# Seven Strassen products for the sv projection, its move to the end of the projections, and rotary swaps and decay powers moved off VectorE

## The chip, the cores and the metric

The kernel runs on one core of one Trainium2 chip. Its time is the device time of one execution in microseconds. The core's engines are TensorE (PE, with its weight loads listed as PEld), VectorE (DVE), ScalarE (ACT), GpSimd (POOL) and SyncE (SP), whose queue issues most transfers. Each works through its own instructions in order and waits for the others at semaphores.

## The reference

The kernel computes one layer of a hybrid encoder for 512 positions of width 1024, in float32. The part that the change touches is the first half of it, the projections, the retention and the spatial gating unit (SGU):

```python
h = rmsnorm(x, g_pre_mix)
q, k, v, g, u, sv, a_ret, a_sgu = split(h @ w_in)     # widths 512, 512, then 1024 each
# rotary, per head of 128 columns (64 + 64)
q = concat([t1 * cos - t2 * sin, t1 * sin + t2 * cos]) # the same for k
# retention, 4 heads, in both directions with decays gamma_f, gamma_b
#   o[n] = sum over m <= n of gamma_f^(n-m) (q[n].k[m]) v[m] + sum over m > n of gamma_b^(m-n) (q[n].k[m]) v[m]
y_ret = (layernorm_per_head(o) * silu(g)) @ w_ret_o
sv = layernorm(gelu(sv))
y_sgu = (gelu(u) * (w_spatial applied to sv per 128 positions + b_spatial)) @ w_sgu_o
x1 = x + rmsnorm((sigmoid(a_ret) * y_ret + sigmoid(a_sgu) * y_sgu) @ w_out)
y = x1 + rmsnorm(conv_gated_mlp(rmsnorm(x1)))
```

## The kernel before

**Products in three matmuls.** Every float32 product is made of three matmuls in a reduced format: each operand is split into a high half, a copy on ScalarE (`copy`, line 95), and a low half, the operand less its high half, on VectorE (`split`, line 112); then high·high, high·low and low·high are added up in a PSUM bank of 128 x 512. There are eight such banks.

**The weights' stream.** `units` lists the weight blocks in the order in which the products want them, written out by hand. `raw_tile` gives one of four tiles of 128 x 1024, which a transfer on the SP queue fills from `wall` (512 KB); `slot` gives one of nine weight slots ("w4") for a half. `w_get` hands out the next unit and prepares later ones as far as its look-ahead (`LOOK`, 4) and the slots allow. A block (`w_block`) is split in one go of 1024 columns. For Strassen products `w_form` (lines 177 to 202) makes forms of 512 columns from two loaded blocks: T1 to T4 are sums and differences in a further raw tile (lines 188, 189, 191, 194), and each form is split into its own slot. The copy on ScalarE and the low half on VectorE stand in the engines' queues among everything else, and a raw tile can be loaded anew when its last reader is done.

**The stages.** First q and k (all eight banks, lines 346 to 376), with x in high and low halves. Their raw results go to SBUF (lines 446 to 452), cos and sin are loaded on the SP queue (lines 468, 469) and scaled on VectorE (470, 471). Then `t_group` (lines 563 to 576) makes one 512-column half of v, sv or g for all four blocks of 128 rows: 4 weight blocks x 4 row blocks x 2 x 3 = 96 matmuls of 128 x 512 (lines 573 to 575), with a `yield` after each weight block. Half 0 of v comes first, beside head 0's preparation. Then the loop over the four heads runs one `t_group` each, interleaved with a head: transposes of k (`k_rows`, line 552), `scores` (line 600), after the first weight block `states`, after the second `prep` of the next head and `values` (line 629), then the other two weight blocks and the evacuation. The groups are v half 1, sv half 0, sv half 1, g half 0. A fifth group makes g half 1; in it the first half of the retention's output, multiplied by its gate, is transposed (`transposed`, line 698), and x's forms for k = 2, 3 are made (`x_forms`, lines 377 to 390). sv's normalization (`sv_norm`, line 685) and the second gate (`g_evac`, lines 707, 708) follow.

**Retention on VectorE.** `rotary` (lines 511 to 517) makes four instructions, two of which read the other 64 partitions (lines 514, 515). `powers` (lines 502 to 508) makes a matrix of decays of 128 x 512 with two VectorE instructions (lines 504, 505) and one exponential on ScalarE, once for `scores` and once for q's factor xi. `o` is normalized per head after a square root on GpSimd (line 657).

**U and the gates.** u comes in four Strassen pairs (class `Pair`, products on line 793): seven products of 12 matmuls with 256 columns for a pair of output blocks, with the products M1 and S2 in one bank, whose content is copied out by ScalarE between them. The first pair takes its products in the order M1, S1, S2, and then the second term of M1's output. The second half of the retention's output is transposed in the first gated pair (`last_turn`, line 715). Gates, output projection and the convolution MLP follow, and are unchanged.

Of the kernel before, what the change touches and what calls it, by code (L numbers as in the profile page):

```python
# [27 lines left out]
U0, GATE0, GATE1 = 32, 40, 72  # L28
# [19 lines left out]
def tile_block(ctx: ExitStack, tc, xT, x, wall, par, cs, wsp, bsp, gpost, gffn, out):  # L48
# [72 lines left out]
    while i < NW:  # L121
        pair = [(f, i) for f in FORMS]
        if U0 <= i < GATE0:
# [17 lines left out]
        else:  # L141
            units.append(("blk", i))
            i += 1
    w_ready, w_pos, w_held, w_raw = {}, [0, 0], [0], {}
# [75 lines left out]

    def w_unit(u):
        return w_block(u[1]) if u[0] == "blk" else (w_down if u[0] in "qt" else w_form)(*u)

    def w_size(u):
        return 2 if u[0] in ("blk", "q", "t") else 1
# [196 lines left out]
    v = nc.vector  # L422
# [57 lines left out]
    (dp, dn), (xp, xn) = halves("dd"), halves("xx")  # L480

    def clip(o, i, op):
        v.tensor_scalar(out=o, in0=i, scalar1=0.0, scalar2=None, op0=op)

    iota(dp.rearrange("p (i n) -> p i n", i=2), [[-P, 2], [1, 256]], 0, -1)
    clip(dn, dp, ALU.min)
    clip(dp, dp, ALU.max)
    iota(xp, [[1, S]], -255, 0)
    iota(xn, [[1, S]], -256, 0)
    clip(xp, xp, ALU.max)  # L490
    clip(xn, xn, ALU.min)
# [10 lines left out]
    def powers(o, p, n, h):  # L502

        v.tensor_scalar(out=o, in0=p, scalar1=lg[:, h : h + 1], scalar2=None, op0=ALU.mult)
        v.scalar_tensor_tensor(
            out=o, in0=n, scalar=lg[:, 4 + h : 5 + h], in1=o, op0=ALU.mult, op1=ALU.add
        )
        nc.scalar.activation(out=o, in_=o, func=AF.Exp)
        return o

    def rotary(m):
        a, b = blk(n="rot"), tmp("rb")
        v.tensor_mul(a, raw[m], cosr)
        v.tensor_mul(b[0:64], raw[m][64:128], sinr[64:128])
        v.tensor_mul(b[64:128], raw[m][0:64], sinr[0:64])
# [21 lines left out]
    def prep(h):  # L537
# [5 lines left out]
        xi = powers(tmp("xi"), xp, xn, h)  # L543
# [56 lines left out]
    def scores(h):  # L600
        (qh, ql), (kh, kl) = hd[h][:2]
        dec = powers(tmp("dec"), dp, dn, h)
# [65 lines left out]
    def sv_evac(acc, nh):  # L668
        for t in range(NT):
            z = blk(n="sv")  # L670
            nc.scalar.activation(
                out=z, in_=acc[t], func=AF.Gelu_apprx_tanh, scale=rstd[:, t : t + 1]
            )
            v.bn_stats(out=sst[:, t, nh, :], in_=z)
            svz[t, nh] = z
        if nh == 1:
            for t in range(NT):
                v.bn_aggr(out=smv[:, t, :], in_=sst[:, t].rearrange("p a b -> p (a b)"))
            rsqrt(srstd, smv[:, :, 1], 1.0, NT)
# [13 lines left out]
    def transposed(src, hi, lo):  # L693

        for f in range(4):
# [7 lines left out]

    def g_evac(acc, nh):
        for t in range(NT):
            g = tmp("g")
            nc.scalar.activation(out=g, in_=acc[t], func=AF.Silu, scale=rstd[:, t : t + 1])
            v.tensor_mul(o_sb[t, nh], o_sb[t, nh], g)

    def last_turn(fs):  # L710

        for f in fs:
            p = ps()
            for t in range(NT):
                i = nc.tensor.transpose(p[:, t * P : (t + 1) * P], o_sb[t, 1][:, f * P : (f + 1) * P], ident)
            h_, l_ = blk(F32R, "gh"), blk(F32R, "gl")
            split(h_, l_, p)
            ogh.append(h_)
            ogl.append(l_)
        return i.ins  # L720
# [9 lines left out]

    for h in range(H):
        gen = t_group()
        k_rows(h)
        sm = scores(h)
        acc = next(gen)
        st = states(h)
        next(gen)
        if h + 1 < H:
# [12 lines left out]
    for n, acc in enumerate(t_group()):  # L751
# [764 lines left out]
```

## Time and profile before

| what | value |
|---|---|
| median of 3 runs | 790.97 us (789.35, 790.97, 791.0) |
| the profiled execution's own time | 791.37 us |
| its span in the profile | 789.6 us |
| granted TensorE clock, mean | 0.997 |
| q and k | to about 47 us |
| v half 0, and heads 0 to 2 with their groups | 48 to 152 us |
| head 3 and the g half 0, then g half 1 | 152.5 to 203 us |
| four U pairs | 203.3 us on |

A row of the groups of lines has the line, engine, operation, output and inputs, shapes and count, then the busy time in us, the mean ns of one and the idle time of the engine ahead of them with its releaser. A row of a timeline has the start and length in us, the engine, line and operation, and in brackets the idle time ahead of it and what ended it. A duration overlaps the next one's start on VectorE, ScalarE and PE, so the time that an instruction takes of its engine is read from start to start. Rows of windows have, after the stretch and its length, the busy time of PE, PEld, DVE, ACT and POOL with the number of instructions, then the granted clock, the share of the DMA engines and GB/s.

### The profile page before, as it was taken

To read this page: it belongs to the slowest core of one execution; us is meant where nothing else is said; L and a number is where in the kernel's file an instruction comes from. 1 tells how busy PE (TensorE), PEld (TensorE's weight loads), DVE (VectorE), ACT (ScalarE), POOL (GpSimd) and SP (SyncE) were. 2 spreads that over 40 slices of the span, in tenths; PEclk is the share of its full clock that TensorE was granted. 3 is DMA by queue.
4 is the path that set the end of the run, shared out by engine and by line. 5 is a ranking of instruction groups with operands and counts; after the bars stand their busy time and mean duration, and the time that the engine had idled before them with its cause. 6 is when DMAs were issued, how large, how long until landed. Compare 5 with 4: busy or idle time off the path is not lost.

```text
span 789.6 us, 13358 instructions
## 1 busy us (share of the span) xinstructions
PE 779.5 (99%) x5163; PEld 724.9 (92%) x5163; DVE 645.1 (82%) x1102; ACT 451.0 (57%) x805; POOL 88.0 (11%) x106
## 2 busy tenths in 40 slices
PE   9999999999999999999999999999999999999996
PEld 8888998998999999999998898999999998999996
DVE  7489998887897777777765669999999889877877
ACT  7546446645676444444444677657777578744442
POOL 0010000110001011032211210001111012200001
PEclk9999999999999999999999999999999999999998
DMA  8733222222233333233359111435555365633244
GB/s 298 264 124 107 80 82 79 81 81 70 104 108 107 107 107 107 86 103 107 134 164 339 59 54 54 116 111 141 141 147 147 108 192 120 168 109 116 99 161 161
DMA packets 33679, 99.54 MB, mean 126 GB/s; under 512 B 3984, under 2 KB 5904, under 8 KB 33616
## 3 DMA queue, kind: packets, MB, share of 16 engines
q1 hardware_dynamic: 27360, 86.76, 32.0%
q0 software_dynamic: 5392, 10.75, 6.4%
q10 hardware_dynamic: 864, 1.18, 0.4%
q8 instruction: 40, 0.66, 0.4%
q14 instruction: 23, 0.19, 0.1%
HBM read 88.19 MB, written 4.19 MB: 117 GB/s over the span
## 4 chain that ended last, share of the span: by engine, by line
PE 80%; DVE 8%; DMA 5%; ACT 3%; issue 2%; POOL 0%; SPq 0%; POOLq 0%; DVEq 0%; ACTq 0%
PE ps L793 23%; PE ps L242 10%; PE ps L241 10%; PE ps L243 10%; PE ps L1210 6%; PE ps L573 5%; PE ps L575 5%; PE ps L574 5%; DMA raw<-wall 3%; DVE dl L112 1%; DMA x<-x 1%; DMA xT<-xT 1%; PE ps L874 1%; PE ps L959 1%; PE ps L958 1%
## 5 line engine op out<-in xcount | busy, mean ns | idle before, releaser
L112 DVE TENSOR_TENSOR wl<-raw,wh 128x1024 fp32r<-128x1024 f32 (+1 forms) x92 | 105.7, 1157 | 41.5 <-PE ps L793 18.9
L95 ACT ACTIVATE wf<-raw 128x512 fp32r<-128x512 f32 x140 | 84.7, 624 | 81.4 <-PE ps L242 29.7
L793 PE MATMUL ps<-sh,wf 128*128 128x256 f32 x640 | 116.6, 275 | 0.0
L112 DVE TENSOR_TENSOR wf<-raw,wf 128x512 fp32r<-128x512 f32 x140 | 101.2, 735 | 18.6 <-ACT wf L95 18.1
L95 ACT ACTIVATE wh<-raw 128x1024 fp32r<-128x1024 f32 (+2 forms) x96 | 93.0, 980 | 24.2 <-DMA raw<-wall 13.1
L793 PEld LDWEIGHTS ps<-sh,wf 128*128 128x128 f32 x640 | 101.7, 192 | 0.5
L242 PE MATMUL ps<-h2l,wh 128*128 128x512 f32 (+1 forms) x256 | 90.2, 354 | 0.7 <-DVE h2l L1031 0.7
L243 PE MATMUL ps<-h2h,wl 128*128 128x512 f32 (+1 forms) x256 | 90.1, 353 | 0.0
L241 PE MATMUL ps<-h2h,wh 128*128 128x512 f32 (+1 forms) x256 | 90.1, 354 | 0.0
L793 PE MATMUL ps<-sl,wf 128*128 128x256 f32 x320 | 88.0, 275 | 0.0
L573 PE MATMUL ps<-wh,xh 128*128 128x512 f32 x192 | 73.0, 380 | 0.0
L574 PE MATMUL ps<-wl,xh 128*128 128x512 f32 x192 | 72.8, 379 | 0.0
L575 PE MATMUL ps<-wh,xl 128*128 128x512 f32 x192 | 72.8, 379 | 0.0
L793 PEld LDWEIGHTS ps<-sl,wf 128*128 128x128 f32 x320 | 61.4, 192 | 0.4
L1210 PE MATMUL ps<-dl,fh 128*128 128x256 f32 x216 | 59.6, 276 | 0.2 <-DVE dl L112 0.2
L1210 PE MATMUL ps<-dh,fh 128*128 128x256 f32 x216 | 59.4, 275 | 0.0
L1210 PE MATMUL ps<-dh,fl 128*128 128x256 f32 x216 | 59.4, 275 | 0.0
L95 ACT ACTIVATE dh<-raw 128x768 fp32r<-128x768 f32 (+1 forms) x36 | 33.6, 949 | 36.0 <-DVE raw L214 21.1
L242 PEld LDWEIGHTS ps<-h2l,wh 128*128 128x128 f32 x256 | 48.6, 190 | 5.4 <-DVE h2l L1031 0.9
L243 PEld LDWEIGHTS ps<-h2h,wl 128*128 128x128 f32 x256 | 48.5, 190 | 5.2
L793 PE MATMUL ps<-xh,wf 128*128 128x256 f32 x288 | 52.8, 277 | 0.0
L241 PEld LDWEIGHTS ps<-h2h,wh 128*128 128x128 f32 x256 | 48.4, 190 | 4.8 <-ACT h2h L1028 0.3
(317 smaller groups left out, 2045.2 us busy)
## 6 DMA issues: line engine op xcount, KB each, us to landing
raw<-wall SPq DMA_DIRECT2D x144, 512.0 KB, 3.5
x<-x SPq DMA_DIRECT2D x24, 256.0 KB, 6.1
fl<-gp POOLq DMA_DIRECT2D x12, 256.0 KB, 3.7
x<-x POOLq DMA_DIRECT2D x8, 256.0 KB, 2.4
fl<-fs POOLq DMA_DIRECT2D x8, 256.0 KB, 3.4
xT<-xT SPq DMA_DIRECT2D x7, 256.0 KB, 5.3
xT<-xT POOLq DMA_DIRECT2D x4, 256.0 KB, 3.3
fl<-gp POOLq DMA_DIRECT2D x8, 128.0 KB, 3.6
```

Source lines behind the costliest of these rows:

```text
L95: return nc.scalar.activation(out=o, in_=i, func=AF.Copy)
L112: nc.vector.tensor_sub(lo, src, as32(hi))
L241: nc.tensor.matmul(o, ah, bh, start=start, stop=False, skip_group_check=skip)
L242: nc.tensor.matmul(o, ah, bl, start=False, stop=False, skip_group_check=skip)
L243: nc.tensor.matmul(o, al, bh, start=False, stop=stop, skip_group_check=skip)
L573: nc.tensor.matmul(acc[t], xh[k][:, c], turns(wh[:, f]), start=k == 0, stop=False)
L574: nc.tensor.matmul(acc[t], xh[k][:, c], turns(wl[:, f]), start=False, stop=False)
L575: part_end[0] = nc.tensor.matmul(acc[t], xl[k][:, c], turns(wh[:, f]), start=False, stop=k == KD - 1)
L793: self.last = nc.tensor.matmul(o, w_[:, c], a_, start=first and k == n == 0, stop=k == 3 and n == 2, skip_group_check=True,)
L874: nc.tensor.matmul(o[:, t * P : (t + 1) * P], svz[t, j // 4][:, (j % 4) * P : (j % 4 + 1) * P], wst[:, gs], start=True, stop=True,)
L958: nc.tensor.matmul(o, ah, turns(bh), start=k == 0, stop=False)
L1210: nc.tensor.matmul(o, a_[:, c], turns(w_[:, f]), start=j == t == i == 0, stop=j == DP - 1 and i == 2 and n not in (M2, M3, M4), skip_group ...
```

## The change

- **sv by Strassen.** sv's 512 x 1024 by 1024 product is made of seven products instead of eight. `sv_group` takes seven products of 24 matmuls with 512 weight columns moving (x's forms are the stationary side): 168 matmuls instead of 192. Each product accumulates into two banks; three times the banks' content is saved by ScalarE and at the end added or subtracted on VectorE (`finish`). The weights' forms (`w_sv`) come from running sums: `s_sum` is loaded from two strided transfers of 256 KB and added to in place, and the forms are split in halves of 512, or 1024 at once for the three that stand in a raw tile.
- **Order.** v half 1, g half 0 and g half 1 come with heads 0 to 2; sv comes with head 3 and after it. g half 1 is kept in SBUF (`gate`) and multiplied after the loop. x's forms for k = 2, 3 come after heads 1 and 2. The transposes of the retention's output stand at three steps of sv's generator, and `last_turn` goes. `sv_norm` comes after the first U pair.
- **Rotary.** The exchange of the two halves of 64 partitions is done by 16 transfers of 128 KB on the SP queue, issued ahead of those of cos and sin, and a rotary has three instructions on VectorE. The sign of sin's table is turned accordingly.
- **Powers.** Distances stay unclipped where all of a block has one sign, and ScalarE makes the power by an exponential with a scale: four of 128 x 128 for a decay matrix, two of which read two small VectorE instructions, and two of 128 x 256 for xi.

```diff
-U0, GATE0, GATE1 = 32, 40, 72
+SV0, U0, GATE0, GATE1 = 24, 32, 40, 72
...
+        if i == SV0:
+            units += [(f, k) for f in ("s11", "sT1", "sT2") for k in range(2)]
+            units += [(f, k) for k in range(2) for f in ("s22", "sT3")]
+            units += [(f, k) for f in ("s21", "sT4") for k in range(2)]
+            i = U0
...
+    def w_sv(form, kp):
+
+        def load(n):
+            raw = raw_tile()
+            nc.sync.dma_start(raw, wall[SV0 + 2 * n + kp])
+            return raw
+
+        def add(raw):
+            for i in range(2):
+                v.tensor_add(s_sum[kp][i], s_sum[kp][i], raw[:, i * S : (i + 1) * S])
+
+        hi, lo = slot("sh"), slot("sl")
+        if form == "s11":
+            s_sum[kp] = halves("sb")
+            for i in range(2):
+                nc.sync.dma_start(s_sum[kp][i], wall[SV0 + kp, :, i * S : (i + 1) * S])
+        elif form == "sT1":
+            add(load(2))
+        elif form == "sT2":
+            s_22[kp] = load(3)
+            add(s_22[kp])
+        elif form == "s22":
+            split(hi, lo, s_22[kp])
+        elif form == "sT3":
+            raw = load(2)
+            v.tensor_add(raw, raw, s_22[kp])
+            split(hi, lo, raw)
+        elif form == "s21":
+            raw = load(1)
+            split(hi, lo, raw)
+            add(raw)
+        if form in ("s11", "sT1", "sT2", "sT4"):
+            for i in range(2):
+                f = slice(i * S, (i + 1) * S)
+                split(hi[:, f], lo[:, f], s_sum[kp][i])
+        return hi, lo
...
+    swapped = []
+    for m in range(8):
+        t = blk(n="swap")
+        for a, b in ((0, 64), (64, 0)):
+            nc.sync.dma_start(t[a : a + 64], raw[m][b : b + 64])
+        swapped.append(t)
...
+    def power(o, e, g):
+        nc.scalar.activation(out=o, in_=e, func=AF.Exp, scale=lg[:, g : g + 1])
+
+    def decays(h):
+
+        w, o = near[:, (2 + h % 2) * P : (3 + h % 2) * P], tmp("dec")
+        v.tensor_scalar(out=w, in0=near[:, :P], scalar1=lg[:, h : h + 1], scalar2=None, op0=ALU.mult)
         v.scalar_tensor_tensor(
-            out=o, in0=n, scalar=lg[:, 4 + h : 5 + h], in1=o, op0=ALU.mult, op1=ALU.add
+            out=w, in0=near[:, P : 2 * P], scalar=lg[:, 4 + h : 5 + h], in1=w, op0=ALU.mult, op1=ALU.add
         )
-        nc.scalar.activation(out=o, in_=o, func=AF.Exp)
+        q = o.rearrange("p (q n) -> p q n", q=4)
+        for i in (0, 3):
+            nc.scalar.activation(out=q[:, i], in_=w, func=AF.Exp)
+        power(q[:, 1], dist[:, 2 * P : 3 * P], h)
+        power(q[:, 2], dist[:, :P], 4 + h)
         return o
 
     def rotary(m):
-        a, b = blk(n="rot"), tmp("rb")
+        a, b = blk(n="rot"), swapped[m]
         v.tensor_mul(a, raw[m], cosr)
-        v.tensor_mul(b[0:64], raw[m][64:128], sinr[64:128])
-        v.tensor_mul(b[64:128], raw[m][0:64], sinr[0:64])
+        v.tensor_mul(b, b, sinr)
         v.tensor_add(a, a, b)
         return a
...
+    def sv_group():
...
+        def finish(n, bank, t0, nh, sub):
+            for t in range(2):
+                a, b = (bank[t], held[n][t]) if sub != "held" else (held[n][t], bank[t])
+                (v.tensor_sub if sub else v.tensor_add)(held[n][t], a, b)
+                gelu(t0 + t, nh, held[n][t])
+
+        b0 = [ps(), ps()]
+        yield from product(b0, x_(0, T0), True, False)
+        save("M1", b0, 0, 0)
+        b2 = [ps(), ps()]
+        yield from product(b2, s_("S1"), True, False)
+        save("M5", b2, 2, 1)
+        yield from product(b0, s_("S2"), False, False)
+        save("U2", b0, 0, 1)
+        for _ in zip(product(b2, s_("S4"), False, True), product(b0, s_("S3"), False, False)):
+            yield
+        finish("U2", b2, 0, 1, "bank")
+        finish("M5", b0, 2, 1, "held")
+        b1 = [ps(), ps()]
+        yield from product(b1, x_(4, T0), True, True)
+        finish("M1", b1, 0, 0, "")
+        yield from product(b0, x_(4, T1), False, True)
...
     for h in range(H):
-        gen = t_group()
+        gen = t_group() if h < 3 else sv_group()
...
-        for _ in gen:
-            pass
-        (v_evac, sv_evac, sv_evac, g_evac)[h](acc, (1, 0, 1, 0)[h])
+        if h < 3:
+            for _ in gen:
+                pass
+            (v_evac, g_evac, g_evac)[h](acc, (1, 0, 1)[h])
+        if h in (1, 2):
+            more_forms(h + 1)
+    for t in range(NT):
+        v.tensor_mul(o_sb[t, 1], o_sb[t, 1], gate[t])
...
-    for n, acc in enumerate(t_group()):
...
-    sv_norm()
-    g_evac(acc, 1)
+    for n, _ in enumerate(gen):
+        if n in (0, 3, 4):
+            transposed([o_sb[t, int(n > 0)] for t in range(NT)], ogh, ogl, {0: range(4), 3: (0, 1), 4: (2, 3)}[n])
     summed = row_sums()
...
+        if j == 0:
+            sv_norm()
```

More of the change, by code (lines that the diff above doesn't have):

```diff
@@ L478, in iota @@
         )
[L480 to L491, printed above, removed]
+    dist, xe = blk(n="dd"), blk(n="xx")
+    near = blk(n="near")
+    iota(dist[:, : 3 * P].rearrange("p (i n) -> p i n", i=3), [[P, 3], [1, P]], -P, -1)
+    for i, op in enumerate((ALU.max, ALU.min)):
+        v.tensor_scalar(
+            out=near[:, i * P : (i + 1) * P], in0=dist[:, P : 2 * P], scalar1=0.0, scalar2=None, op0=op
+        )
+    iota(xe.rearrange("p (i n) -> p i n", i=2), [[257, 2], [1, 256]], -256, 0)
     ze = const("ze", [P, NT])
@@ L601, in scores @@
         (qh, ql), (kh, kl) = hd[h][:2]
-        dec = powers(tmp("dec"), dp, dn, h)
+        dec = decays(h)
         sm = []
@@ L691, in tile_block, with transposed @@
     ogh, ogl = [], []
-    def transposed(src, hi, lo):
-        for f in range(4):
+    def transposed(src, hi, lo, fs=range(4)):
+        for f in fs:
             p = ps()
@@ L702, in transposed @@
             lo.append(l_)
+    gate = []
     def g_evac(acc, nh):
         for t in range(NT):
-            g = tmp("g")
+            g = blk(n="g") if nh else tmp("g")
             nc.scalar.activation(out=g, in_=acc[t], func=AF.Silu, scale=rstd[:, t : t + 1])
[L708 to L720, printed above, removed]
+            if nh:
+                gate.append(g)
+            else:
+                v.tensor_mul(o_sb[t, 0], o_sb[t, 0], g)
     def row_sums():
```

93 lines of the change are left out of this document (56 added, 37 removed).

## The prediction, made before the changed kernel was run

> **What bounds the kernel now.** First the engines' shares on the page, then TensorE's (PE's) list of waits, its first and its last row of five.
>
> ```profile
> PE 779.5 (99%) x5163; PEld 724.9 (92%) x5163; DVE 645.1 (82%) x1102; ACT 451.0 (57%) x805; POOL 88.0 (11%) x106
> ```
> ```profile
> PE ps L343 <- PEq L1506: 0.8, 1, 0.8
> ...
> PE ps L793 <- ACT c L95: 0.2, 1, 0.2
> ```
>
> PE is busy 99% of the span, and no row of its waits is over 0.8 us: between the first matmul and the last one the time is the sum of PE's instructions. Work taken from PE shortens the kernel, as long as the engines that feed it keep up. Whether they do is read by stage, so I took the busy time of each engine in two stretches (columns: us, then PE, PEld, DVE, ACT, POOL busy, each with its instructions; granted clock; DMA): from head 2's values to the first U pair, and the U pairs.
>
> ```profile
> 138.30:200.10 61.80, 61.80 (x344) 55.62 (x343) 50.51 (x98) 34.92 (x56) 7.26 (x12) 1.00 0.24 82
> 203.40:250.00 46.60, 46.60 (x411) 46.36 (x410) 42.11 (x73) 31.05 (x59) 4.37 (x3) 1.00 0.33 109
> ```
>
> VectorE (DVE) has 50.5 us of work in the first 61.8 us, and 42.1 in the next 46.6: 11.3 and 4.5 us to spare. PE is the bound, with DVE close behind it.
>
> **What PE saves.** Two rows of PE's timeline, eleven matmuls of 512 columns apart:
>
> ```profile
> 49.48 0.38 PE L573 MATMUL ps<-wh,xh 128*128 128x512 f32 x1
> ...
> 51.85 0.38 PE L575 MATMUL ps<-wh,xl 128*128 128x512 f32 x1
> ```
>
> 2.37 us over 11 is 0.2157 us each. sv's two halves are 2 x 96 = 192 of them now and 7 x 24 = 168 after: 24 x 0.2157 = **5.2 us less**. All other matmuls and transposes stay; 16 transposes of the retention's second half come ahead of the U pairs instead of into the first gated pair.
>
> ```profile
> 185.52 1.91 PE L698 MATMUL ps<-ident,o 128*128 128x128 f32 x16
> ```
> ```profile
> 203.28 0.27 PE L793 MATMUL ps<-xh,wf 128*128 128x256 f32 x1
> ...
> 205.85 0.39 PE L793 MATMUL ps<-sh,wf 128*128 128x256 f32 x2
> ```
>
> Sixteen such take 1.7 us when the last one's tail under the next matmul (0.2) is left off. So U's first product can begin at 203.28 - 5.2 + 1.7 = 199.8, and the third product (S2), whose first matmul is the second of the row at 205.85 (205.96), 2.68 us later: at 202.5. At the end of the first gated pair PE would be 5.2 us ahead.
>
> **What DVE gains and loses.** Slots are taken from start to start, since durations in DVE's timeline overlap the next instruction:
>
> ```profile
> 223.30 0.68 DVE L188 TENSOR_TENSOR raw<-raw 128x512 f32<-128x512 f32 x1
> 223.91 0.69 DVE L112 TENSOR_TENSOR wf<-raw,wf 128x512 fp32r<-128x512 f32 x1
> ```
> ```profile
> 139.13 1.23 DVE L112 TENSOR_TENSOR wl<-raw,wh 128x1024 fp32r<-128x1024 f32 x1
> 140.27 0.68 DVE L112 TENSOR_TENSOR k<-rot,k 128x512 fp32r<-128x512 f32 x1
> ```
> ```profile
> 147.97 1.39 DVE L657 TENSOR_SCALAR o<-o,mv,orstd 128x256 f32<-128x256 f32 x4 [1.19 <-POOL orstd L403]
> 149.27 1.22 DVE L112 TENSOR_TENSOR wl<-raw,wh 128x1024 fp32r<-128x1024 f32 x1
> ```
>
> So 0.60 us for 512 elements, 1.14 for 1024, 0.33 for 256 (four in 1.30). What goes, by the groups of lines:
>
> ```profile
> L514 DVE TENSOR_TENSOR rb<-qkraw,cs 64x512 f32<-64x512 f32 x8 | 5.5, 687 | 0.2
> L504 DVE TENSOR_SCALAR xi<-xx,lg 128x512 f32<-128x512 f32 x4 | 1.9, 484 | 0.1
> L505 DVE SCALAR_TENSOR_TENSOR xi<-xx,lg,xi 128x512 f32<-128x512 f32 x4 | 3.0, 751 | 0.0
> ```
>
> A rotary has two half-height products of 0.69 (lines 514, 515) and gets one full one: 8 x (1.38 - 0.60) = 6.2 us. Two powers per head, 0.40 + 0.66 each: 8.5 us, less two 128-wide instructions per head, which by the 256-wide row cost at most 8 x 0.33 = 2.6. About 12 us go, nearly all in heads 0 to 2, where they come too early to be kept: DVE can only work ahead as far as the nine weight slots allow. What comes is in sv: 28 adds and low halves of 512 and 8 of 1024 make 16.8 + 9.1 = 25.9 us where eight low halves of 1024 made 9.1, and six adds at the banks' end 3.6: **20 us more**, nearly all behind head 2.
>
> **Where that shows: a chain, followed through the changed order of instructions.** In head 2's group a low half of an sv form (sl, line 112) waits for a weight slot that PE leaves at the end of the group's second block, before the values:
>
> ```profile
> 138.10 0.27 PE L241 MATMUL ps<-vh,sm 128*128 128x256 f32 x1
> ```
>
> From there, about 138.3, to the low half of the first U pair's T3 DVE has 107 instructions, in order. 71 have 512 elements: 26 of sv's forms, 6 adds and 4 statistics of sv, 4 gate products, 8 low halves of the turned output, 8 for the U forms, 15 for head 3 and the rest. 8 have 1024, 20 have 256, and 8 are aggregates:
>
> ```profile
> L652 DVE BATCH_NORM_AGGREGATE mv<-bs 128x2 f32<-128x6 f32 x16 | 2.7, 177 | 0.3
> ```
>
> 71 x 0.60 + 8 x 1.14 + 20 x 0.33 + 8 x 0.1 = 59.1 us, against the 50.5 of the same stretch now. Idle time of DVE: two waits for GpSimd's square root at 1.19 (row at 147.97), 2.4, is the least; now it is 11.3, the most. I take 4.5, near the lower end, because a DVE that is behind finds its inputs ready. The chain ends at 138.3 + 59.1 + 4.5 = 201.9. It frees the raw tile for the second pair's load, which is issued at 200.12 now:
>
> ```profile
> 200.12 0.33 SPq L181 DMA_DIRECT2D raw<-wall  x1
> ```
> ```profile
> raw<-wall SPq DMA_DIRECT2D x144, 512.0 KB, 3.5
> ```
> ```profile
> 204.90 0.38 ACT L95 ACTIVATE u<-ps 128x256 f32<-128x256 f32 x1
> 205.16 0.64 ACT L95 ACTIVATE wf<-raw 128x512 fp32r<-128x512 f32 x1
> ```
>
> It lands at 205.4. ScalarE's copy of that block (0.6) stands in its queue **ahead of** the copy of U's first product (0.38), and S2 accumulates into that product's bank, so it waits for the copy: until 206.3 (the two overlap by 0.1, as in the rows above), where PE is ready at 202.5. **A stall of 3.8 us** (now the copy ends 0.7 us before it is needed). With the least idle it is 1.7, with 6 us of idle 5.3.
>
> Behind it the U pairs get sv's normalization:
>
> ```profile
> L685 DVE TENSOR_SCALAR sv<-sv,smv,srstd 128x512 f32<-128x512 f32 x8 | 4.0, 537 | 1.2 <-POOL srstd L403 1.2
> ```
>
> 8 x 0.45 = 3.6 us, against 4.5 to spare. Further waits of PE there lie between nothing and those 3.6; I take 0.9, the low side, since DVE works ahead during the stall.
>
> **The swaps.** Sixteen transfers of 128 KB stand on the SP queue ahead of the loads of cos and sin.
>
> ```profile
> 50.76 0.42 SPq L468 DMA_DIRECT2D cs<-cs  x1
> 51.24 0.42 SPq L469 DMA_DIRECT2D cs<-cs  x1
> ```
> ```profile
> 54.87 0.69 DVE L470 TENSOR_TENSOR cs<-cs,rbc 128x512 f32<-128x512 f32 x1 [2.44 <-DMA cs<-cs]
> ```
> ```profile
> 68.90 0.60 PE L552 MATMUL ps<-ident,rot 128*128 128x128 f32 x4
> ```
> ```profile
> fl<-gp POOLq DMA_DIRECT2D x8, 128.0 KB, 3.6
> ```
> ```profile
> x<-x SPq DMA_DIRECT2D x24, 256.0 KB, 6.1
> ```
>
> At 0.48 each they take 7.7 us of the queue; one raw load (some 3 us) goes behind them, so cos lands near 59.5 and sin near 60, 5 us later than now. Head 0's rotary and its parts need 7 us of DVE from there, to 67.4, and PE asks for them at 68.9: 1.5 us of cover, cost **nothing**, if a swap lands like the nearest row in size (3.6). If it lands like the loads of x (6.1), each transfer also waiting for the one eight before it on the same lane, cos comes 4.5 us later: a wait of 3 us. DVE's 2.4 us wait for cos grows to some 7, in which it only loses lead.
>
> **Powers and the rest.** ScalarE gets six small exponentials per head for two of 512, beside 35 us of work in 61.8: nothing, bounded by a late decay matrix, 1 us. Moved forms of x, gate products and transposes are in the chain's count.
>
> **Sum.** Profiled 791.4 (span 789.6); the runs' median is 791.0, and the difference of 0.4 is their scatter, so changes are taken from 790.97. -5.2 + 3.8 + 0.9 = -0.5: **790.5 us**.
>
> **A rule that speaks against it.** The granted clock (next to last but two) after PE's last matmul, near 782.0:
>
> ```profile
> 782.00:784.00 2.00, 0.00 (x0) 0.00 (x0) 2.00 (x7) 0.78 (x4) 0.60 (x1) 1.00 0.34 132
> 784.00:786.00 2.00, 0.00 (x0) 0.00 (x0) 1.80 (x4) 0.00 (x0) 0.33 (x1) 0.86 0.69 267
> ```
> ```profile
> 0.76 3.49 PE L343 MATMUL ps<-const-bfloat16-1.0 128*128 128x256 bf16 x17 [0.76 <-PEq L1506]
> ```
>
> A mean of 0.86 between 1.00 and 0.50 means that the clock halved 1.44 us into the second stretch, some 3.4 us after PE fell idle; and at the start 17 matmuls of 256 columns took 3.49 us, 0.205 each, where they take 0.11 later: about 3.5 us at half speed, a loss of 1.7. The Trainium skill, "TensorE: Matmul & The Clock Gate", Part 1, says the same (half clock after an idle window of about 3.4 us, full clock after as long of work) and adds that the window runs freely, so that an idle stretch just over it need not hold a whole one; the trace agrees with the length, and no run here shows the free running.
>
> **Rivals.**
> - *The cover holds*: the chain ends 2 us or more earlier, or the second pair's tile lands before ScalarE reaches it. For it: 11.3 us of DVE idle now; against: 8.6 us more work. Without a stall 785.8, with 2 us of it and the 0.9 788.7.
> - *The clock falls, slower*: at S2 of the first U pair. It decides when PE's stall passes 3.4 us by enough to halve the clock; the price is 1.7 on top. At a stall of 3.8 that is 792.2, at 5.3 793.7. For it: my stall is at that edge; against: one observation of the edge, and no stall over 0.8 now.
> - *Swaps late*: +3, 793.4.
> - *The relief doesn't come*: ScalarE's queue, in which the small exponentials stand between copies, delays DVE by as much as DVE was spared; the chain's idle is 6 or more, and U is bound by DVE (3.6): 791.0 - 5.2 + 5.3 + 3.6 = 794.7 at most.
>
> **Chances.** A measurement tells 0.2% (1.6 us) from no change: 789.4 and 792.6. Forecast (stall 2 to 5, no lower clock, 788.7 to 791.7) 0.42: faster 0.14, same 0.26, slower 0.02. Cover holds 0.26, faster. Clock 0.16: slower 0.13, same 0.03. Swaps 0.10, slower. No relief 0.06: slower 0.05, same 0.01. In all faster 0.40, same 0.30, slower 0.30. The range leaves out the ends of the outer cases: 786.2 to 793.6.
>
> **What would show it.** Right: PE's waits get one row of 3 to 4 us at line 793's counterpart, released by ScalarE's copy of u, with SP's load behind DVE's low half of T3 near 202; U's first matmul near 199.8; 168 matmuls at 0.2157. Wrong: no such row (then 786); the granted clock under 1.00 near 207; a wait of PE near 69 on k or q; DVE idle on ScalarE in heads 1 to 3.

## The result and the profile after

The changed kernel takes 794.89 us (median of 4 runs, 793.6 to 795.35) and the kernel before 790.43. The measured ratio is 1.0046, with a 95% interval of 1.0033 to 1.0059: some 3.6 us **slower** (the two medians by themselves are 4.5 us apart). Forecast were 790.5 us and a range of 786.2 to 793.6. (The medians of the kernel before lie between 790.4 and 791.5 us from one comparison to the next; below, kernels are compared by their ratios to it, and 0.1% is 0.8 us. Profiles are of single executions; their start-up differs by up to 2.3 us (head 0's first transposes begin between 68.2 and 70.5 us), so that stretches are measured from head 3 or from U's first product.)

The page's first lines, and the first rows of PE's waits:

```profile
span 793.5 us, 13415 instructions
...
PE 778.5 (98%) x5139; PEld 723.2 (91%) x5139; DVE 647.9 (82%) x1118; ACT 460.7 (58%) x840; POOL 90.7 (11%) x105
```
```profile
PE ps L901 <- ACT u L95: 3.5, 1, 3.5
PE ps L901 <- ACT sig L95: 1.6, 1, 1.6
PE ps L388 <- PEq L1610: 0.8, 1, 0.8
PE ps L806 <- ACT o L95: 0.6, 1, 0.6
```

PE has 24 matmuls fewer and is busy only 1.0 us less, where 5.2 were saved. Two waits are new, both in Strassen pairs (line 901) and both for a copy on ScalarE. PE's timeline around the first, in the first U pair:

```profile
201.29 0.27 PE L901 MATMUL ps<-xh,wf 128*128 128x256 f32 x1
...
204.19 0.28 PE L901 MATMUL ps<-xh,wf 128*128 128x256 f32 x1
207.92 0.58 PE L901 MATMUL ps<-sh,wf 128*128 128x256 f32 x1 [3.46 <-ACT u L95]
208.30 0.42 PE L901 MATMUL ps<-sl,wf 128*128 128x256 f32 x1
```

U begins at 201.29 (203.28 before), S2 at 207.92 (205.96 before). The matmuls behind the wait are longer. The windows over the same stretch (the clock is the third number from the end):

```profile
204.00:206.00 2.00, 0.46 (x5) 0.27 (x3) 2.00 (x4) 1.99 (x5) 0.00 (x0) 1.00 0.76 254
206.00:208.00 2.00, 0.08 (x1) 0.08 (x1) 2.00 (x4) 1.76 (x4) 0.00 (x0) 0.61 0.02 8
208.00:210.00 2.00, 2.00 (x9) 2.00 (x10) 1.64 (x7) 0.00 (x0) 1.34 (x2) 0.50 0.71 244
210.00:212.00 2.00, 2.00 (x11) 2.00 (x11) 1.43 (x3) 0.90 (x2) 0.53 (x1) 0.50 0.09 27
212.00:214.00 2.00, 2.00 (x14) 2.00 (x14) 2.00 (x5) 1.15 (x2) 0.00 (x0) 0.68 0.00 0
```

The granted clock halved at 206.44 (a mean of 0.61 is 0.44 us at 1.00 and 1.56 at 0.50) and came back at 213.28. VectorE's last low half of the chain, T3's, and the load that it releases:

```profile
202.69 0.68 DVE L112 TENSOR_TENSOR wf<-raw,wf 128x512 fp32r<-128x512 f32 x1
```
```profile
203.39 0.33 SPq L188 DMA_DIRECT2D raw<-wall  x1
```

That is 203.4, forecast 201.9. ScalarE's timeline up to the copy of U's first product (the copy is the last row):

```profile
202.20 1.33 ACT L756 ACTIVATE sv<-sv,rstd 128x512 f32<-128x512 f32 x2 [1.99 <-DVE sv L762]
203.44 1.25 ACT L756 ACTIVATE sv<-ps,rstd 128x512 f32<-128x512 f32 x2
204.58 0.59 ACT L95 ACTIVATE rws<-ps 128x512 f32<-128x512 f32 x1
205.19 2.41 ACT L95 ACTIVATE wf<-raw 128x512 fp32r<-128x512 f32 x4
207.50 0.37 ACT L95 ACTIVATE u<-ps 128x256 f32<-128x256 f32 x1
```

ScalarE waited 2 us for VectorE's adds of sv (line 762), and then did four gelus, the row sums' copy and four weight forms without a pause before it came to u. The second new wait, at the first gated pair, with ScalarE and GpSimd ahead of it:

```profile
248.22 0.38 PE L901 MATMUL ps<-sh,wf 128*128 128x256 f32 x1 [1.65 <-ACT sig L95]
```
```profile
242.72 0.63 ACT L95 ACTIVATE wf<-raw 128x512 fp32r<-128x512 f32 x1 [2.56 <-POOL raw L197]
```
```profile
239.28 3.41 POOL L197 TENSOR_TENSOR raw<-raw,raw 128x512 f32<-128x512 f32 x1 [28.74 <-ACT wf L95]
```

**Account between the two profiled executions** (PE's starts). Head 3 begins at 153.10 for 152.48: +0.6, of which 0.5 is a wait for q and k in head 0. From there to U's first product 48.2 us for 50.8: -2.6, where -3.5 was forecast; 0.6 of the rest is the wait for the retention's output at the transposes. S2: +3.6 for the wait and +2.6 for the clock until 213.3. The 16 transposes that are gone from the first gated pair: -1.6. The wait for sig: +1.7. Together +4.3; PE's last matmul starts 4.3 us later, and the span is 3.9 longer since the end is a little shorter.

### The profile page after: what moved, and what is told of

It reads as the page before. It is cut to its first block, busy times and chain, and to the rows that moved or that the text cites. A ratio compares the mean times of both kernels' runs of the same rounds, so it can differ in the third digit from the quotient of the medians.

```text
span 793.5 us, 13415 instructions
## 1 busy us (share of the span) xinstructions
PE 778.5 (98%) x5139; PEld 723.2 (91%) x5139; DVE 647.9 (82%) x1118; ACT 460.7 (58%) x840; POOL 90.7 (11%) x105
## 4 chain that ended last, share of the span: by engine, by line
PE 63%; DVE 16%; DMA 7%; ACT 6%; issue 5%; POOL 1%; SPq 1%; POOLq 0%; DVEq 0%; ACTq 0%
PE ps L901 22%; PE ps L287 9%; PE ps L286 9%; PE ps L288 9%; DMA raw<-wall 4%; PE ps L1314 3%; PE ps L629 2%; PE ps L630 2%; PE ps L628 2%; DVE dl L112 2%; DVE sl L112 1%; PE ps L1064 1%; PE ps L1063 1%; PE ps L1062 1%; ACT wh L95 1%
## 5 line engine op out<-in xcount | busy, mean ns | idle before, releaser
L112 DVE TENSOR_TENSOR wl<-raw,wh 128x1024 fp32r<-128x1024 f32 (+1 forms) x84 | 95.8, 1150 | 46.6 <-PE ps L901 15.7
L901 PE MATMUL ps<-sh,wf 128*128 128x256 f32 x640 | 118.7, 278 | 5.1 <-ACT u L95 3.5
L95 ACT ACTIVATE wh<-raw 128x1024 fp32r<-128x1024 f32 (+2 forms) x88 | 84.7, 974 | 31.9 <-DMA raw<-wall 15.3
L1314 PE MATMUL ps<-dh,fh 128*128 128x256 f32 x216 | 59.5, 275 | 0.0
L630 PE MATMUL ps<-wh,xl 128*128 128x512 f32 x128 | 48.5, 379 | 0.0
L629 PE MATMUL ps<-wl,xh 128*128 128x512 f32 x128 | 48.5, 379 | 0.0
L628 PE MATMUL ps<-wh,xh 128*128 128x512 f32 x128 | 48.5, 380 | 0.0
```

Of the source, the lines that this page charges most:

```text
L95: return nc.scalar.activation(out=o, in_=i, func=AF.Copy)
L112: nc.vector.tensor_sub(lo, src, as32(hi))
L628: nc.tensor.matmul(acc[t], xh[k][:, c], turns(wh[:, f]), start=k == 0, stop=False)
L629: nc.tensor.matmul(acc[t], xh[k][:, c], turns(wl[:, f]), start=False, stop=False)
L630: part_end[0] = nc.tensor.matmul(acc[t], xl[k][:, c], turns(wh[:, f]), start=False, stop=k == KD - 1)
L901: self.last = nc.tensor.matmul(o, w_[:, c], a_, start=first and k == n == 0, stop=k == 3 and n == 2, skip_group_check=True,)
```

## The experiments

Seventeen kernels were run, e1 to e22 with gaps in the numbers. All start from the changed kernel unless said. A measure that tells the kernels apart is the time from the start of U's first product to the start of ScalarE's copy of it: 1.62 us in the kernel before, 6.21 in the changed one. How long the granted clock stays at half behind S2's wait differs from profile to profile: not at all in e1, 3.4 us in e3, e5, e11, e13, e14 and e15, 6.8 us in the changed kernel, e7, e16 and e21. A difference of a microsecond or two between two of these kernels can come from that alone; the last section says what decides it.

**First theory: VectorE is late from head 3 to the end of U, and what it has too much shows up as time, a us for a us.** Rival: the order of a few instructions at U's start is the cause.

### e1: u's copy ahead of the second pair's B21

```diff
-            o = self.product(0, self.x(0, T0), True)
+            o = self.product(0, self.x(0, T0), True, w_get(3.5) if apart else None)
```

> Only ScalarE's order at the first U pair changes: the copy of U's first product goes ahead of the high half of the second pair's B21. Theory (VectorE is late over the whole of sv and U, and the stall at S2 is where it shows): the stall of 3.5 us and the lower clock behind it go, but VectorE, with only some 3 us idle between 205 and 250 us, hands most of it back as waits at later pairs: 791.9 to 793.4 us against 794.9. Rival (the order of two copies is the whole cause): 794.9 - 3.5 - 2.6 = 788.8, with no new wait over 1 us in U.

794.61 us, ratio 1.0042 (1.0029 to 1.0055): no change that can be told. ScalarE's timeline, and the window in which PE stood still:

```profile
205.73 1.67 ACT L95 ACTIVATE wf<-raw 128x512 fp32r<-128x512 f32 x3
207.31 0.36 ACT L95 ACTIVATE u<-ps 128x256 f32<-128x256 f32 x1
207.57 0.62 ACT L95 ACTIVATE wf<-raw 128x512 fp32r<-128x512 f32 x1
```
```profile
205.00:207.00 2.00, 0.00 (x0) 0.00 (x0) 2.00 (x5) 1.99 (x5) 0.00 (x0) 1.00 0.72 260
```

The B21 form is behind the copy now, but the copy starts 5.48 us after U's first product instead of 6.21: the tile of the second pair, on which the prediction's stall rested, was worth **0.7 us** of 3.5. Three other forms still stand ahead. PE stood idle 3.06 us and the clock stayed at 1.00; even so, from U's first product to the first product of the retention's output it took 50.5 us against 51.1, since later waits took up most of the difference (2.4 us for sig, 0.5 for u, 0.4 for a form). The rival as it was put (two copies) falls, and the clock's 2.6 us were not lost on top.

### e3: sv's normalization after the fourth U pair

```diff
-        if j == 0:
+        if j == 3:
             sv_norm()
```

> sv's normalization (8 VectorE instructions, 3.6 us) comes after the fourth U pair instead of the first. Theory: the stall at S2 (3.5 us) and the lower clock stay, and PE's wait of 1.6 us at the end of U goes: 793.2 us. Rival (that wait is ScalarE's own, not VectorE's lateness): 794.9, the wait stays.

793.89 us, ratio 1.0031 (1.0022 to 1.0040). The wait for sig fell to 0.5 us, as expected, but the wait for u's copies grew to 4.4 in two places; about 1 us came of the 1.7 that the theory expected.

### e5: the Strassen products without the relief

The rotary's and the powers' code of the kernel before, and no swaps.

> The Strassen products alone: rotary and powers stand on VectorE as in the kernel before, without the 16 swaps, some 12 us more of VectorE's work, most of it in heads 0 to 2. Theory (the relief comes too early to be kept): the low half of the first pair's T3 ends at most 1.5 us later than 203.4, and the shift of 0.6 us in head 0 goes: 794.3 to 796.5 us. Rival (the relief reaches U): 12 us more of work show up as 6 us or more, over 800.

796.64 us, ratio 1.0062 (1.0050 to 1.0075): 0.16% over the changed kernel, just past the theory's end and far from the rival's. The theory's first part fails, though. T3's low half ends at 206.65, 3.3 us later, where at most 1.5 was expected:

```profile
205.97 0.68 DVE L112 TENSOR_TENSOR wf<-raw,wf 128x512 fp32r<-128x512 f32 x1
```

PE waits 3.0 us in head 3, for st and kz, and U's first product begins 51.5 us after head 3, against 48.2 in the changed kernel. So the relief does reach U's start. In U 1.7 us came back (49.4 us to the first product of the retention's output, for 51.1), where the clock was low for 3.4 us instead of 6.8. In time the relief is worth about 1.3 us in this order.

### e7: sv's running sums on GpSimd

```diff
-                v.tensor_add(s_sum[kp][i], s_sum[kp][i], raw[:, i * S : (i + 1) * S])
+                nc.gpsimd.tensor_tensor(out=s_sum[kp][i], in0=s_sum[kp][i], in1=raw[:, i * S : (i + 1) * S], op=ALU.add)
```

> The 12 running sums of sv's weight forms (512 elements each) are added on GpSimd instead of VectorE, 7.2 us of VectorE's slots. Theory: T3's low half ends near 197, the second pair's tile is there in time, the stall at S2, the lower clock and the wait at the end of U go: 786 to 787.5 us, faster than both kernels. Rival (VectorE is not what sets it, or GpSimd's adds come late and PE waits for sv's forms): 790 or more, with waits of PE in sv's products.

801.95 us, ratio 1.0127 (1.0111 to 1.0143): the rival. GpSimd's first add:

```profile
136.53 1.60 POOL L238 TENSOR_TENSOR sb<-sb,raw 128x512 f32<-128x512 f32 x1 [5.54 <-DVE sl L112]
```

1.6 us where VectorE takes 0.60. VectorE, in order, then stands at the sums and is late with what follows: ahead of U, PE waits 1.4 us for st, 1.2 for kz, 1.1 for sv's low halves and 1.8 for its adds (line 762), and in U 5.4 for u. VectorE's work went down by 7.2 us and the kernel got slower, which is the first sign against "a us for a us".

### e6: the relief alone

The kernel before with swaps and powers as in the changed kernel.

> The kernel before with the rotary's swaps by transfers and the powers on ScalarE, without the Strassen products: some 12 us less of VectorE's work and the same work of PE. Theory (VectorE's early time isn't what PE waits for, and the sixteen swaps delay cos and sin by 8 us): no gain; PE's shift of 0.6 us in head 0 stays: 0.2 to 1.0 us slower than before. Rival (the relief is a gain by itself): 0.5 us faster or more.

791.44 us, ratio 1.0004 (0.9993 to 1.0015): no gain, no loss. VectorE's work does not count where PE is the bound. The swaps cost nothing by themselves: heads 0 to 1 take 27.86 us in both profiles.

### e8: the retention's normalization on ScalarE (heads 2 and 3)

```diff
+            if h > 1:
+                nc.scalar.activation(
+                    out=ot, in_=ot, func=AF.Identity, scale=orstd[:, h, n : n + 1], bias=onb[:, h, n : n + 1]
+                )
+                continue
```

> The changed kernel with the normalization of the retention's output of heads 2 and 3 on ScalarE: eight VectorE instructions (2.6 us) and VectorE's two waits for GpSimd's square root (2.6 us) leave the chain, ScalarE gets eight of 0.38 us. Theory (VectorE's lateness sets sv and U, a us for a us): VectorE reaches T3's low half near 198.5 and the wait at S2 shrinks to under 1 us; 2.5 to 5 us faster than the changed kernel, that is within 1.5 us of the kernel before. Rival (ScalarE's queue is what is late at U): its 3 us more make it no faster, 4 us over the kernel before or more.

799.01 us, ratio 1.0099 (1.0080 to 1.0117): the rival again. The first rows of PE's waits:

```profile
PE ps L911 <- ACT u L95: 3.9, 4, 2.9
PE ps L746 <- ACT sv L95: 2.7, 1, 2.7
```

ScalarE now waits for GpSimd's square root, and behind it stand the copies that free sv's banks: PE waits 2.7 us in the middle of sv, where VectorE's wait had cost PE nothing, and the clock is at half for 3.4 us behind it, from 184.17.

### e11: cos and sin loaded ahead of the swaps

```diff
+    cosr, sinr = halves("cs")
+    nc.sync.dma_start(cosr, cs[0])
+    nc.sync.dma_start(sinr, cs[1])
     swapped = []
```

> The changed kernel with cos and sin loaded ahead of the sixteen swaps. Theory: VectorE's wait for cos in head 0 shrinks, PE's shift of 0.6 us in head 0 goes, and nothing of VectorE's earlier time reaches head 3: 0.4 to 1.0 us faster than the changed kernel, 3 us over the kernel before. Rival (the late cos is where the relief is lost, and VectorE carries it to U): 3 us faster or more.

796.30 us, ratio 1.0061 (1.0049 to 1.0073): neither. Heads 0 to 1 still took 28.2 us, and behind the wait for sig (2.1 us) the clock fell a second time, from 248.64 to 252.05, where pairs of matmuls stand 0.43 us apart. The order of the loads isn't what costs.

### e13: six more VectorE instructions

```diff
+        for _ in range(6):
+            v.tensor_add(near, near, near)
```

> The changed kernel with six more VectorE instructions of 512 elements (3.6 us) on an unused tile, spread over head 3. Theory (VectorE has no time to spare from head 3 to the end of U): the six show up nearly whole, 2.5 to 3.6 us slower than the changed kernel. Rival (the loss comes from the order of a few copies and loads, and VectorE has room): under 1 us.

793.97 us, ratio 1.0035 (1.0022 to 1.0048): **not slower**. The theory falls. (Four of the six ran between 160 and 174 us; from 160 to 177 us the changed kernel leaves VectorE idle for 3.4 us, from there to T3's low half for nothing. Two ran at 185 and 188, so the run says little about that last stretch.) T3's low half and u's copy:

```profile
204.05 0.68 DVE L112 TENSOR_TENSOR wf<-raw,wf 128x512 fp32r<-128x512 f32 x1
```
```profile
207.42 0.37 ACT L95 ACTIVATE u<-ps 128x256 f32<-128x256 f32 x1
```

VectorE's chain ends 1.4 us later, and u's copy 0.1 us earlier: with other timings the program's order came out with the B21 form behind u.

### e14 and e15: VectorE's work left out

```diff
-    for t in range(NT):
-        v.tensor_mul(o_sb[t, 1], o_sb[t, 1], gate[t])
```

> The changed kernel with the four products of the retention's second half with its gate left out (four VectorE instructions, 2.4 us, in the stretch between head 3's normalization at 177 us and U, where VectorE has no idle time). Nothing is waited for in their place. Theory (VectorE's work between 177 us and the end of U sets the time; the six added instructions of the earlier run fell for the most part ahead of 177 us): T3's low half ends 2.4 us earlier, near 201, and the kernel is 1.5 to 2.5 us faster than the changed one. Rival (ScalarE's queue sets U's start, whatever VectorE does): under 0.7 us.

794.06 us, ratio 1.0035 (1.0022 to 1.0048): 0.9 us less than the changed kernel, short of the theory and a little over the rival, with intervals that overlap. u's copy:

```profile
207.76 0.38 ACT L95 ACTIVATE u<-ps 128x256 f32<-128x256 f32 x1
```

2.4 us less of VectorE's work bring T3's low half to 202.8 and u's copy nowhere. These two kernels leave out a part of the layer and serve for timing only. In e15 `sv_norm()` is left out too:

> As the run without the gate products, and sv's normalization is left out too: eight more VectorE instructions, 3.6 us, between U's first and second pair. Theory: the two together, 6.0 us of VectorE's work, give 4 us or more, so that the kernel is level with the kernel before or up to 1.5 us over it. Rival (U is not bound by VectorE): as the run without the gate products, within 0.7 us.

793.19 us, ratio 1.0026 (1.0014 to 1.0038): 6 us less work bring about 1.6 us, far from the theory's 4 and at the edge of the rival (0.7 us by the ratios under e14, 0.9 by the medians). The wait for sig is gone (e14 had a wait of 1.7 for u in its place), the one at S2 is 3.7. That points to **two limits**: something other than VectorE's amount of work holds S2, and VectorE holds a part of the rest of U.

### e16: four small repairs, without touching the queue ahead of u

cos and sin first, B21 behind u's copy, sv's normalization in the first gated pair, and its T2 on VectorE.

> A version of the changed kernel, with all of its work: cos and sin loaded ahead of the swaps, the copy of U's first product ahead of the second pair's B21, sv's normalization in the first gated pair, and the T2 form of the first gated pair on VectorE (0.6 us) instead of GpSimd (3.4 us there, and ScalarE's queue stood behind it for 2.6). Theory: U loses 3.6 us of VectorE's work and the wait for sig, and head 0 its 0.6 us: 2.5 to 4 us faster than the changed kernel, level with the kernel before within 1.5 us. Rival (the wait moves to the first gated pair, where the normalization is now): as the changed kernel.

794.12 us, ratio 1.0036 (1.0023 to 1.0049). That is 0.8 us faster than the changed kernel, the rival's number, but not for its reason: the wait for sig is gone and none came in its place, and S2 still waits 3.1 us, with the clock low for 6.8 us.

### e17, e20, e21: what stands ahead of u's copy

In e17 the copy of U's first product goes ahead of the two gelus of sv's last product, the row sums' copy (both put off in `sv_rest`), and of T3, T4, B22 and what follows them (a shorter look-ahead at sv's last products).

```diff
-                wh, wl = w_get()
+                wh, wl = w_get(2 if near_u else LOOK)
...
-            o = self.product(0, self.x(0, T0), True)
-            copy(two(c0[:, T0]), o)
+            o = self.product(0, self.x(0, T0), True, w_get(2) if apart else None)
+            i = copy(two(c0[:, T0]), o)
+            if apart:
+                with tc.issue_after(i.ins):
+                    for f in sv_rest:
+                        f()
+                    w1 = w_get()
```

> The changed kernel, all work kept; on ScalarE the two gelus of sv's last product, the copy of the row sums and the high halves of the first pair's T3, T4 and B22 stand behind the copy of U's first product instead of ahead of it. The runs so far have S2 at 207.7 to 208.3 us whether VectorE had 2.4 us less or 3.6 us more work before it, which speaks for ScalarE's queue as what sets S2, and their ends differ, which speaks for VectorE as what sets the rest of U. Theory of two limits: the wait at S2 falls below 1 us and the granted clock stays at 1.00 there, but VectorE takes most of it back at later pairs: 0.5 to 2.5 us faster than the changed kernel. Rival (S2's wait and the clock behind it are the whole cost): 4 us faster or more, level with the kernel before.

789.81 us, ratio **0.9983 (0.9972 to 0.9993)**: 5 us better than the changed kernel, and 1.3 us faster than the kernel before. ScalarE's timeline, and the first row of PE's waits:

```profile
201.28 1.15 ACT L95 ACTIVATE wf<-raw 128x512 fp32r<-128x512 f32 x2 [0.53 <-DVE raw L197]
202.46 0.38 ACT L95 ACTIVATE u<-ps 128x256 f32<-128x256 f32 x1
202.74 1.26 ACT L758 ACTIVATE sv<-ps,rstd 128x512 f32<-128x512 f32 x2
```
```profile
PE ps L906 <- ACT wf L95: 0.9, 1, 0.9
```

u's copy starts 1.54 us after U's first product, S2 waits 0.1 us, and the clock stays at 1.00. The rival of that expectation holds: S2's wait with what follows from it was the cost. e20 puts only the forms behind u's copy:

> One half of the repair in e17: only the first pair's T3, T4 and B22 (and the second pair's first forms) are prepared after the copy of U's first product; sv's last two gelus and the row sums' copy stay ahead of it. Theory (what is late is the forms that VectorE sums, with the low halves that stand ahead of M1's adds in VectorE's own order): the copy ends near 204.5, the wait at S2 is under 1 us and the kernel is within 1 us of e17. Rival (the gelus count as much): half of e17's gain, S2 waits 1.5 us or more.

793.53 us, ratio 1.0022 (1.0013 to 1.0031): 1.9 us better than the changed kernel and 3.1 behind e17, so the time fits neither. The rows of PE's waits:

```profile
PE ps L901 <- DVE wf L112: 1.8, 3, 1.4
PE ps L507 <- ACT qkraw L95: 1.2, 1, 1.2
PE ps L901 <- ACT u L95: 1.1, 2, 0.6
PE ps L901 <- ACT sig L95: 1.0, 1, 1.0
PE ps L901 <- ACT wf L95: 0.9, 1, 0.9
```

The copy starts 3.04 us after U's first product and S2 waits 0.6, as the theory had it. But VectorE's order came out otherwise than in e17: sv's normalization, which waits for GpSimd's square root, stands ahead of the forms' low halves.

```profile
208.44 1.00 DVE L793 TENSOR_SCALAR sv<-sv,smv,srstd 128x512 f32<-128x512 f32 x2 [1.44 <-POOL srstd L448]
```

So the low halves are late (1.4 of the 1.8), and the second pair's tile is loaded at 210.07 instead of 206.36 (the 0.9). Whether the place of the gelus brought that order about isn't shown. e21 puts only the gelus and the row sums behind:

> The other half: sv's last two gelus and the row sums' copy go behind the copy of U's first product, the forms stay ahead of it. Theory: T4's form and the high half of the second pair's B21, whose tile lands near 207, still stand ahead, S2 waits 2.5 us or more and the kernel is at most 1.5 us faster than the changed one. Rival (the gelus are the block): within 1 us of e17.

793.96 us, ratio 1.0031 (1.0021 to 1.0042): as the theory had it. ScalarE waits for T4, which VectorE has added only by 205:

```profile
205.04 2.19 ACT L95 ACTIVATE wf<-raw 128x512 fp32r<-128x512 f32 x4 [1.70 <-DVE raw L200]
207.13 0.36 ACT L95 ACTIVATE u<-ps 128x256 f32<-128x256 f32 x1
```

So neither half is enough. The forms ahead of u hold S2 (6.06 us to the copy with the gelus gone); once they are behind it, it matters when their low halves come, and in e20, with another order on VectorE, more than half of the gain was lost.

### e18, e19: what VectorE still holds

e18 is e17 with cos and sin first, the normalization in the first gated pair and T2 on VectorE.

> As the run with u's copy first, and cos and sin ahead of the swaps, sv's normalization in the first gated pair, and the T2 form of the first gated pair on VectorE. All work kept. Theory of two limits: with VectorE's 3.6 us out of U and ScalarE's queue cleared, both limits move: 3 to 6 us faster than the changed kernel, that is from 1 us over the kernel before to 2 us under it. Rival (only S2 counts): as the run with u's copy first.

789.68 us, ratio 0.9985 (0.9972 to 0.9998), as e17: those repairs add nothing that can be told. e19 leaves the gate products and the normalization out:

> As the run before it in this call, but with the four gate products and sv's normalization left out (6.0 us of VectorE's work in all). Theory of two limits: VectorE no longer holds U, PE's saving of 5.2 us appears nearly whole: 3 us or more under the kernel before. Rival (a further limit, the transfers of the raw tiles or GpSimd): within 1 us of the kernel before, with waits of PE in U that VectorE doesn't explain.

787.62 us, ratio 0.9958 (0.9945 to 0.9970), 3.3 us under the kernel before. The four U pairs take 38.7 us from the first start to the gated pair's, against 40.6 in e17 and 37.5 for four of 9.38: with VectorE's 6 us gone (this kernel too leaves out a part of the layer) two waits are left there, 0.5 us together, both within ten microseconds of U's start. VectorE is the second limit, and it costs e17 about 2 us of PE's 5.2.

### e22: e17's order without the relief

> e17's order, but rotary and powers on VectorE as in the kernel before, without the swaps (some 12 us more of VectorE's work, most of it in heads 0 to 2). Theory (the relief comes too early for U): at most 2 us slower than e17, level with the kernel before. Rival (the relief is what carries the Strassen products): 4 us slower than e17 or more.

793.42 us, ratio 1.0023 (1.0014 to 1.0032): 0.40%, 3.2 us, behind e17, between the two expectations. Once the queue ahead of u is mended the relief counts. The price of doing without it lies ahead of U, as in e5: PE waits 3 us in head 3 for st and kz, and U's first product begins 51.5 us after head 3, against 48.2 in e17. From there the two are level (46.6 and 46.5 us to the first product of the retention's output), although ScalarE's wait of 1.7 us for VectorE's T2 keeps its form and u's copy back to 206.4.

A fifth raw tile, which would take the second pair's load out of the chain directly, wasn't tried.

## Why the prediction was wrong, point by point

- **PE's saving**: right. 168 matmuls at 0.2157 us; the 5.2 us appear as 3.3 in e19, where little else is in the way.
- **The swaps**: the cost taken, nothing, holds within 0.5 us (e6: 1.0004), but the cover was used up. The sixteen took 11.53 us of SP's queue instead of 7.7 (0.58 each in the median, and 2.2 us of waiting for q's and k's raw results, which the sum left out), and VectorE's product with cos began at 62.70 instead of some 59.5:

```profile
48.03 11.53 SPq L501 DMA_DIRECT2D swap<-qkraw  x16
```
```profile
62.70 0.69 DVE L520 TENSOR_TENSOR cs<-cs,rbc 128x512 f32<-128x512 f32 x1 [1.58 <-DMA cs<-cs]
```

- **U's start**: 0.9 us of waits on the way weren't counted, 0.6 of them at the transposes.
- **VectorE's chain**: right in size. 64.6 us from 138.76 to 203.37, 59.9 of them busy; forecast were 63.6 and 59.1.
- **The stall at S2**: right in place, and in size by luck, 3.5 us for 3.8. The step that puts ScalarE's copy of the second pair's block ahead of u's copy, with a tile that lands at 205.4, names one of the instructions ahead of u, and that one was worth 0.7 us (e1). The gelus of sv's last products, which wait for VectorE's adds, the row sums and the forms T4 and B22 stand in the same queue. The forms alone hold S2 for 3.6 us (e21), the gelus and the row sums alone for 0.6 (e20). The prediction followed one chain and didn't list the queue ahead of u's copy instruction by instruction, though it named the queue.
- **The clock**: the step that failed most. "It decides when PE's stall passes 3.4 us" was read off one place, the end of the kernel. In the nineteen profiles that fall at the end comes between 2.2 us (e7) and 5.3 us (e17) after PE's last matmul, so the 3.4 read there was one case of many. Here the clock fell 2.0 us after PE's last matmul at 204.46 and stayed low for 6.8 us; the price in the profile was 2.6 us, not 1.7. The chance of 0.16 was too small. Of the four runs, the one with a mean clock of 0.998 took 793.6 us, the three with 0.994 or 0.995 took 794.9 to 795.4.
- **Later waits in U**: 0.9 taken, 1.7 measured, by way of GpSimd's T2, which took 3.4 us (1.8 before), and ScalarE's queue behind it.
- **The sum**: -5.2 + 0.6 + 0.9 + 3.5 + 2.6 + 1.7 = +4.1, for the -0.5 forecast; the profiles differ by 3.9. The terms aren't independent: with the clock at 1.00 (e1) the wait for sig grew from 1.6 to 2.4 and others appeared, and the time was the same. What comes behind S2's wait, the clock and the later waits together, was put at 0.9 us and measured 4.3.
- **"The relief comes too early to be kept"**: wrong. Without the relief U begins 3.3 us later in both orders (e5, e22). In the changed kernel's order 1.3 us of that shows in the time, in e17's order 3.2.
- What the experiments leave open: which of VectorE's instructions between 177 us and the gated pair cost e17 its last 2 us, and why e11 is slower than the changed kernel in U by more than its second fall of the clock.

## What to carry to other kernels

When a product's bank is reused, look up the copy that frees it and list everything that stands ahead of it in its engine's queue, together with what each of these waits for: here four gelus, a copy and four weight forms, of which some waited for another engine and others were for later products, cost 5 us, enough to turn a gain into a loss. Moving that one copy forward was worth more than 6 us of another engine's work (e17 against e15). An experiment that only removes work from the engine that looks late tells less than one that changes the order.

## What the runs showed of the hardware

- **The clock's window.** The clock fell at 206.44 and rose at 213.28, 6.83 us apart. In every profile the changes of the granted clock that the trace records lie whole multiples of 3.413 us apart: here 59 of them from the first rise to the fall, then 2 to the rise. So the clock changes only at the ends of windows of that length, which follow one another whatever PE does, and PE's idle time within a window decides. Cut into these windows, the nineteen profiles have no exception up to PE's last matmul: the clock fell after each of the 14 windows with 1.99 us or more of idle time, and after none of some 4300 with 1.93 or less. At half, it stayed there after windows with 0.7 us or more and rose after windows with 0.24 or less. A stall therefore counts by how it lies on the windows. In e1 the 3.06 us fell into two, 1.93 and 1.1, and the clock never fell. In e16 3.05 us fell into two as 2.02 and 1.04, and it was at half from 205.44 to 212.27:

```profile
204.00:206.00 2.00, 0.00 (x0) 0.00 (x0) 2.00 (x4) 1.99 (x4) 0.00 (x0) 0.86 0.58 227
206.00:208.00 2.00, 1.52 (x7) 1.53 (x8) 2.00 (x8) 0.94 (x3) 0.12 (x1) 0.50 0.16 29
```

 The Trainium skill, "TensorE: Matmul & The Clock Gate", Part 1, has a window of 3413 ns that runs freely and doesn't start anew with the kernel; the traces agree with that. Its advice to avoid idle gaps above some 3.4 us is too wide by these runs: the wait of 2.09 us in e11 was enough.
- **GpSimd's add of 128 x 512** took between 1.27 and 2.80 us in e7, 1.53 in the median (0.60 on VectorE). The T2 form of the first gated pair took 3.41 us in the changed kernel and 1.28 in e17; in the kernel before it took 1.80:

```profile
232.45 1.80 POOL L191 TENSOR_TENSOR raw<-raw,raw 128x512 f32<-128x512 f32 x1 [51.28 <-ACT u L95]
```

 What makes the difference wasn't tried.
- **Swaps between partitions** of SBUF, 128 KB on 64 partitions, took 0.58 us each of the queue in the median and landed after 2.3 us; the loads of cos and sin, 256 KB each, took 0.42 us of the queue in the kernel before.
